# A decoder trunk on one core: conditioning units taken in groups of two to four, with projection granules between their loads and their matmuls

## The chip, the core and the metric

The kernel runs on one core of a Trainium2 chip. A core has five engines that run side by side and wait for each other through semaphores: TensorE (PE in the profile; its weight loads are PEld), VectorE (DVE), ScalarE (ACT), GpSimd (POOL) and SyncE (SP), which here issues most DMA transfers. The metric is the device time of one execution in microseconds (us), lower is better. Times are medians of several runs; the profile shows one execution.

## What is computed

One step of a decoder layer for 256 prompt tokens and 8 sequences of 4 sample tokens, 288 token columns in all, width 2048, in fp32. A vector `c` for each sequence (9 in all) conditions the layer:

```python
mod = jax.nn.silu(c) @ P['w_ada'] + P['b_ada']
sh1, sc1, gt1, sh2, sc2, gt2 = [m[:, None, :] for m in jnp.split(mod, 6, axis=-1)]
xn = rmsnorm(x, P['g_norm1']) * (1.0 + sc1) + sh1
mix, st = mixer(xn, states[l], P)
x = x + gt1 * mix
xn = rmsnorm(x, P['g_norm2']) * (1.0 + sc2) + sh2
x = x + gt2 * (jnp.square(jax.nn.relu(xn @ P['w_ff1'])) @ P['w_ff2'])
```

`w_ada` is 2048 x 12288, so 100 MB are read for a product with nine rows. The mixer projects `xn` with `w_in` and splits the result among three branches: RG-LRU (a convolution, gates and a scan), GLA (gated linear attention with a state for each head) and mLSTM (a matrix memory for each head). Their outputs go through `w_br_*`, are weighted by sigmoid gates, summed, and projected by `w_out`. The MLP follows.

## The kernel before

**Layout.** Features lie on the partitions, tokens on the free axis. A k-tile is 128 features by 288 tokens.

**Projections.** `stream` (lines 146 to 169) multiplies one block of 512 output features. It is a generator with one step for each granule of two k-tiles: one load of 0.5 MB into a `raw` tile (line 153, issued by SP), a cast to a rounded `hi` on ACT (154), the remainder `lo` on DVE (155), and 24 matmuls: for 4 output tiles and 2 k-tiles the products hi by xh, hi by xl, lo by xh (161 to 163), in the reduced-width format fp32r. `raw`, `hi` and `lo` have three tiles each. A block holds four PSUM banks, and its `evac` empties them.

**Conditioning.** `cond_product` (lines 205 to 222) multiplies rows of a weight matrix as the moving operand with the nine columns of silu(c) as weights, in plain fp32. One unit is a load of up to 2048 columns of one k-tile (1 MB for `ada`; 0.75 MB for the shift product) and its matmuls (line 216), four at 32 columns of the array each, so that the four column groups of the array work on four parts of the output. A unit's tile comes from `raw_tile` (198): a list `slots["ids"]` names the big slots that are free in the stage, with `None` for a tile of its own. At the end of a product the result is transposed on DVE (193) and finished by small vector operations at high priority.

`fillers` (272) strings the products together: the second half of SC1, SH1, `shift_product` (249; what SH1 adds to the three projection blocks that were run before it was there), GT1, SH2, SC2, GT2. `run` (171) takes a projection's generator through its granules and after some of them takes one step of `fillers`, by the pattern `pace["every"]`: (1,) after every granule, (1, 0) after every second, (1, 0, 0) after every third, () never. One step is one unit: its load and its matmuls. `drain` (283) takes steps until a product is done.

**Order of the stages.** Norm 1 and the first half of SC1; three blocks of `B_Q` over the first eight k-tiles, then over the last eight (lines 395 to 400, a step per granule); `drain("sh")` and the addition of the shift (401 to 403); the fourth block and two blocks for RG-LRU (406 to 410, every second granule); RG-LRU (442 to 508); a narrow stream of 8 granules and two gate blocks (512 to 523); `drain("cor")` (722); GLA (572 on); the first merge (every third granule) and two blocks `B_MX`; mLSTM; the second merge (no steps); two blocks `B_MO`, the third merge and the output projection (every third granule); norm 2; the MLP. The order of instructions on each engine is laid out ahead of time by a scheduler with a timing model: what comes first in the program has priority, and what is not ready is passed by what is. Loads and casts of `stream` have high priority, so they run ahead as far as their tiles allow. Each engine, and SP with its loads, then takes its instructions strictly in that order.

Of the kernel before, what the change touches and what calls it, by code (L numbers as in the profile page):

```python
# [25 lines left out]
NPRE = 3  # blocks of the projections before sh1  # L26

# name -> width of the constant (by shape only) and parameter columns
# [19 lines left out]
# blocks of 512 columns in the packed input projection  # L48
# [4 lines left out]
def trunk(ctx, tc, io):  # L53
# [35 lines left out]
    # ---- constants, parameters  # L89
# [25 lines left out]
    def resets(t, val, one, step):  # L115
        """scan coefficients: val where a segment starts (each step prompt tokens; each sample), one elsewhere"""
        G.memset(t, one)
        G.memset(t[:, 0:NP:step], val)
        G.memset(t[:, NP:N:TS], val)
        return t  # L120

    def head_bcast(p, r, w=N):
        """p[:, h * w ...] for one head at a time: the head's row of r on all partitions"""
# [4 lines left out]
    # ---- streamed weights  # L128
# [3 lines left out]
    def weight_tile(kind):  # L132
        """1024 columns: of the kind's ring, or what stands in for it: a slot or a tile of the states' ring"""
# [12 lines left out]
    def stream(w, blk, act, kt, evac, g0=0, width=512, ahead=True, k0=0):  # L146
        """k-tiles k0..kt-1; act: k -> (hi, lo); generator with a step per granule"""
# [30 lines left out]
    # ---- conditioning: silu(c) @ w_ada + b_ada  # L178
# [4 lines left out]
    silc = cp.tile([P, KT * 9 + 23], F32, tag="silc", name="silc")  # 9 columns a k-tile; read 32 at a time  # L183
# [6 lines left out]
    def by_feature(ps, h, n):  # L190
        """up to eight k-tiles' columns from the column groups: k-tile, 32 columns"""
# [4 lines left out]
    slots = {"ids": (None,), "n": 0}  # L196

    def raw_tile():
        slots["n"] += 1
        i = slots["ids"][slots["n"] % len(slots["ids"])]  # L200
        if i is None:
            return ring.tile([P, 2048], F32, tag="ag", name=nm("ag"))
        return flat(slot(i))[:, 0:2048]

    def cond_product(load, each, cols, stat, finish):
        """columns of w (natural order) times 9 columns of stat (k -> AP of 32 columns): features m * 128 + 32 j + f in the
        array's column group j; a load brings what each of some k-tiles takes"""
        ps = pa.tile([P, 512], F32, tag="pa", name=nm("pa"))
        for q in range(KT // each):
            raw = raw_tile()  # L210
            load(raw, q)
            for i in range(each):
                k = each * q + i
                v = raw[:, cols * i:cols * i + cols].rearrange("p (m j f) -> p j m f", j=4, f=32)
                for j in range(4):
                    T.matmul(ps[32 * j:32 * j + 32, 0:cols // 4], stat(k), v[:, j], start=k == 0, stop=k == KT - 1)  # L216
            if q < KT // each - 1:
                yield
# [5 lines left out]
    def ada_finish(kind):  # L224
        def finish(h, pv):
            o = mod[:, kind, 8 * h:8 * h + 8, :]
            V.tensor_tensor(out=o, in0=pv[:, :, 0:9], in1=bada[:, kind, 8 * h:8 * h + 8].unsqueeze(2).to_broadcast([P, 8, 9]), op=ALU.add)
            if kind in (SC1, SC2):  # g * (1 + sc)
# [9 lines left out]
    def ada(kind):  # L238
        def load(raw, k):
            Q.dma_start(raw.rearrange("p (h m) -> p h m", h=2), wada[kind, :, k].rearrange("h p m -> p h m"))  # L240
        return cond_product(load, 1, 2048, silu_c, ada_finish(kind))

    def ada_half(kind, h):
        """eight of the k-tiles of one kind"""
        def load(raw, q):
            Q.dma_start(raw.rearrange("p (k m) -> p k m", k=2), wada[kind, h, 2 * q:2 * q + 2].rearrange("k p m -> p k m"))
        return cond_product(load, 2, 1024, silu_c, lambda _, pv: ada_finish(kind)(h, pv))

    def shift_product(dst, nb):
        """the tiles of dst += sh1 @ w_in's nb blocks, for each token by its sequence"""  # L250
        def load(raw, k):
            Q.dma_start(raw[:, 0:512 * nb].rearrange("p (b m) -> p b m", b=nb),
# [33 lines left out]

    fill = fillers()

    # ---- normalisation over the features (on partitions and tiles)
    def sumsq(ps, x, k, s):  # L290
        """ps += the squares of x summed over its features; s gathers those of the first twelve k-tiles"""
# [19 lines left out]
    def smp(a):  # the samples' columns, by sequence  # L311
        return a[..., NP:N].rearrange("p k (b t) -> p k b t", b=NB)

    def modulate(xg, rs, k0, fk, xh, xl, xr):
        """k-tiles k0..k0+3 of x (xg) -> hi and lo of x * rstd * f"""
# [945 lines left out]
```

## Time and profile before

| | us |
|---|---|
| median of 3 runs | 2061.9 |
| lowest, highest | 2055.35, 2066.22 |
| the profiled execution, span from its first to its last instruction | 2058.2 |

The profile gives for the profiled execution no time besides its span, so the median is set against that. How to read its rows: a row of the timeline has the start in us, the duration, the engine, the line of the kernel, the operation, the tile written and the tiles read, the shape, and how many instructions of that kind were merged into the row. A bracket at its end says how long the engine had been idle and what ended that. Matmul rows overlap, since the next one starts while the last one is in flight, so starts say more than durations. One fp32 matmul leaves two records, so a unit of four matmuls shows as x8. Tile names: `pa` is the conditioning product in PSUM, `ag` and `s` the tiles its loads go to, `silc` the silu(c) columns, `mod` the SH1 columns, `mm` a projection's PSUM bank, `xh`, `xl` the two parts of the activations.

### The profile page before, as it was taken

To read this page: it belongs to the slowest core of one execution; us is meant where nothing else is said; L and a number is where in the kernel's file an instruction comes from. 1 tells how busy PE (TensorE), PEld (TensorE's weight loads), DVE (VectorE), ACT (ScalarE), POOL (GpSimd) and SP (SyncE) were. 2 spreads that over 40 slices of the span, in tenths; PEclk is the share of its full clock that TensorE was granted. 3 is DMA by queue.
4 is the path that set the end of the run, shared out by engine and by line. 5 is a ranking of instruction groups with operands and counts; after the bars stand their busy time and mean duration, and the time that the engine had idled before them with its cause. 6 is when DMAs were issued, how large, how long until landed. Compare 5 with 4: busy or idle time off the path is not lost.

```text
span 2058.2 us, 35340 instructions
## 1 busy us (share of the span) xinstructions
PE 2000.3 (97%) x14834; PEld 1824.4 (89%) x14834; DVE 1031.4 (50%) x1406; ACT 802.4 (39%) x1099; POOL 302.0 (15%) x342
## 2 busy tenths in 40 slices
PE   6999999999999999999999999999999999999997
PEld 4778778877889788889998989999999999999997
DVE  4354655354644366454444465434545444454565
ACT  3323465332435332244333344444343434343434
POOL 0120111021202223101111242101010101010102
PEclk8999999999999999999999999999999999999999
DMA  9988685377663257777778755555555555555552
GB/s 386 356 316 308 207 298 180 132 243 265 213 235 126 83 187 233 250 251 272 246 252 303 235 187 162 166 170 166 166 163 167 167 166 164 166 165 168 166 167 98
DMA packets 120959, 429.60 MB, mean 209 GB/s; under 512 B 11600, under 2 KB 13808, under 8 KB 120672
## 3 DMA queue, kind: packets, MB, share of 16 engines
q1 hardware_dynamic: 111728, 393.59, 56.4%
q0 software_dynamic: 7920, 29.04, 4.0%
q10 hardware_dynamic: 1152, 4.72, 0.6%
q8 instruction: 116, 1.90, 0.4%
q14 instruction: 43, 0.35, 0.0%
HBM read 410.49 MB, written 16.81 MB: 208 GB/s over the span
## 4 chain that ended last, share of the span: by engine, by line
PE 78%; DMA 2%; DVE 1%; issue 1%; POOL 1%; ACT 0%; DVEq 0%; SPq 0%; POOLq 0%
PE mm L161 24%; PE mm L163 23%; PE mm L162 23%; PE pa L216 3%; DMA st<-mC 1%; DMA ag<-wada 1%; DVE lo L155 0%; PE px L658 0%; PE pi L974 0%; PE px L931 0%; PE pi L535 0%; PE px L125 0%; PE px L980 0%; PE px L555 0%; DMA o_C_s<-st 0%
## 5 line engine op out<-in xcount | busy, mean ns | idle before, releaser
L155 DVE TENSOR_TENSOR lo<-raw,hi 128x1024 fp32r<-128x1024 f32 (+1 forms) x424 | 543.0, 1283 | 616.9 <-ACT hi L154 603.7
L154 ACT ACTIVATE hi<-raw 128x1024 fp32r<-128x1024 f32 (+1 forms) x424 | 442.9, 1046 | 801.5 <-PE mm L162 663.2
L161 PE MATMUL mm<-xh,hi 128*128 128x288 f32 x2168 | 645.4, 300 | 12.0 <-ACT xh L341 5.5
L162 PE MATMUL mm<-xl,hi 128*128 128x288 f32 x2168 | 641.3, 297 | 1.2 <-DVE xl L342 1.2
L163 PE MATMUL mm<-xh,lo 128*128 128x288 f32 x2168 | 630.2, 297 | 1.2 <-DVE lo L155 1.2
L161 PEld LDWEIGHTS mm<-xh,hi 128*128 128x128 f32 x2168 | 406.9, 188 | 67.5 <-issue 37.8
L163 PEld LDWEIGHTS mm<-xh,lo 128*128 128x128 f32 x2168 | 404.6, 189 | 13.4 <-issue 8.1
L162 PEld LDWEIGHTS mm<-xl,hi 128*128 128x128 f32 x2168 | 408.5, 188 | 8.8 <-issue 6.9
L162 PE MATMUL mm<-s,hi 128*128 128x288 f32 x1176 | 348.1, 296 | 0.0
L161 PE MATMUL mm<-s,hi 128*128 128x288 f32 x1176 | 347.6, 297 | 0.0
L163 PE MATMUL mm<-s,lo 128*128 128x288 f32 x1176 | 345.0, 295 | 0.0
L161 PEld LDWEIGHTS mm<-s,hi 128*128 128x128 f32 x1176 | 220.6, 188 | 13.6 <-issue 11.8
L163 PEld LDWEIGHTS mm<-s,lo 128*128 128x128 f32 x1176 | 220.9, 188 | 2.4 <-issue 2.2
L162 PEld LDWEIGHTS mm<-s,hi 128*128 128x128 f32 x1176 | 221.3, 188 | 1.2 <-issue 0.9
L1102 POOL TENSOR_TENSOR t<-t 128x288 f32<-128x288 f32 x64 | 62.6, 989 | 638.9 <-ACT t L1101 638.9
L161 PE MATMUL mm<-s,st 128*128 128x288 f32 x488 | 143.9, 296 | 0.0
L162 PE MATMUL mm<-s,st 128*128 128x288 f32 x488 | 143.3, 294 | 0.0
L154 ACT ACTIVATE st<-s 128x1024 fp32r<-128x1024 f32 x80 | 84.7, 1059 | 131.0 <-PE mm L162 86.9
L161 PE MATMUL mm<-xh,st 128*128 128x288 f32 x408 | 120.5, 297 | 0.2 <-DVE xl L1088 0.2
L162 PE MATMUL mm<-xl,st 128*128 128x288 f32 x408 | 120.1, 295 | 0.0
L161 PEld LDWEIGHTS mm<-s,st 128*128 128x128 f32 x488 | 91.7, 188 | 0.8 <-ACT t L296 0.8
L162 PEld LDWEIGHTS mm<-s,st 128*128 128x128 f32 x488 | 91.9, 188 | 0.0
(369 smaller groups left out, 2104.6 us busy)
## 6 DMA issues: line engine op xcount, KB each, us to landing
raw<-win SPq DMA_DIRECT2D x192, 512.0 KB, 4.4
raw<-wf SPq DMA_DIRECT2D x176, 512.0 KB, 3.4
ag<-wada SPq DMA_DIRECT2D x57, 1024.0 KB, 6.1
s<-wf SPq DMA_DIRECT2D x80, 512.0 KB, 3.5
s<-wada SPq DMA_DIRECT2D x39, 1024.0 KB, 8.3
raw<-wout SPq DMA_DIRECT2D x32, 512.0 KB, 4.4
s<-win SPq DMA_DIRECT2D x11, 768.0 KB, 7.2
st<-mC POOLq DMA_DIRECT2D x16, 514.0 KB, 4.6
```

The source lines that it names most:

```text
L154: S.activation(hi, raw, AF.Copy)
L155: V.tensor_tensor(out=lo, in0=raw, in1=hi.bitcast(F32), op=ALU.subtract)
L161: T.matmul(pss[m][:, :N], hi[:, kk, ms], xh, start=k == k0, stop=False)
L162: T.matmul(pss[m][:, :N], hi[:, kk, ms], xl, start=False, stop=False)
L163: T.matmul(pss[m][:, :N], lo[:, kk, ms], xh, start=False, stop=k == kt - 1)
L216: T.matmul(ps[32 * j:32 * j + 32, 0:cols // 4], stat(k), v[:, j], start=k == 0, stop=k == KT - 1)
L1102: G.tensor_tensor(out=r, in0=r, in1=r, op=ALU.mult)
```

## The change

`cond_product` no longer takes one unit per step. It takes `slots["group"]` units at once: it issues their loads, the last unit's first, so that the load of the unit whose matmuls come first is the last one; then it yields `slots["after"]` times, that is, it lets so many steps pass (granules of projections, where each takes a step); then it issues the matmuls of all the units in order. With `after` 0 it yields behind each unit as before. A new function `feed` sets tiles, group and distance for what follows and first lets a group whose loads have been issued finish.

```diff
-    slots = {"ids": (None,), "n": 0}
+    slots = {"ids": (None,), "n": 0, "group": 1, "after": 0, "loaded": False, "done": 0}
...
         if i is None:
-            return ring.tile([P, 2048], F32, tag="ag", name=nm("ag"))
-        return flat(slot(i))[:, 0:2048]
+            return [ring.tile([P, 2048], F32, tag="ag", name=nm("ag"))]
+        if i == "st":
+            return [sp.tile([P, 1028], F32, tag="st", name=nm("st"), bufs=2)[:, 0:1024] for _ in range(2)]
+        return [flat(slot(i))[:, 0:2048]]
...
-        for q in range(KT // each):
-            raw = raw_tile()
-            load(raw, q)
-            for i in range(each):
-                k = each * q + i
-                v = raw[:, cols * i:cols * i + cols].rearrange("p (m j f) -> p j m f", j=4, f=32)
-                for j in range(4):
-                    T.matmul(ps[32 * j:32 * j + 32, 0:cols // 4], stat(k), v[:, j], start=k == 0, stop=k == KT - 1)
-            if q < KT // each - 1:
+        q = 0
+        while q < KT // each:
+            n = min(slots["group"], KT // each - q)
+            raws = [raw_tile() for _ in range(n)]
+            for i in reversed(range(n)):
+                load(raws[i], q + i)
+            slots["loaded"] = True
+            for _ in range(slots["after"]):
+                yield
+            for raw in raws:
+                for i in range(each):
+                    k = each * q + i
+                    w = cols // len(raw)
+                    for h, r in enumerate(raw):
+                        v = r[:, w * i:w * i + w].rearrange("p (m j f) -> p j m f", j=4, f=32)
+                        for j in range(4):
+                            T.matmul(ps[32 * j:32 * j + 32, h * w // 4:(h + 1) * w // 4], stat(k), v[:, j], start=k == 0 and h == 0,
+                                     stop=k == KT - 1, skip_group_check=len(raw) > 1)
+                q += 1
+            slots["loaded"] = False
+            slots["done"] += 1
+            if not slots["after"] and q < KT // each:
                 yield
...
+    def feed(ids, group, after):
+
+        slots.update(ids=ids, group=group, after=after)
+        n = slots["done"]
+        while slots["loaded"] and slots["done"] == n:
+            next(fill, None)
```

A tile named `"st"` is a pair of tiles of the ring that GLA and mLSTM load their states into; such a unit has two loads and eight matmuls of half the width.

The settings along the program:

```diff
-    slots["ids"] = 2, 5, 6, 7, None
+    slots.update(ids=(2, 5, 6, 7, None), group=2, after=2)
...
-    pace["every"] = (1, 0)
-    slots["ids"] = 6, 7, None
+    feed((0, 1, 3, 4, 5, 6, 7, None), 4, 3)
...
+    drain("cor")
+    feed((6, 7, "st", None), 4, 4)
...
+    pace["every"] = ()
     run(stream(io["wsm"], 0, act1, KT, lambda m, p: S.copy(sm, p), width=P))
+    pace["every"] = (1,)
...
-    drain("cor")
-    slots["ids"] = None,
+    pace["every"] = ()
+    feed((None,), 1, 0)
     ygla = gla()
...
-    pace["every"] = (1, 0, 0)
     merge(0, ylru, io["wbl"])
...
     merge(1, ygla, io["wbg"])
-    pace["every"] = (1, 0, 0)
+    pace["every"] = (1, 0, 0, 0)
...
-    slots["ids"] = 8, 9, None
+    feed((8, 9, None), 3, 4)
+    pace["every"] = (1,)
...
-    for _ in range(3):
-        next(fill, None)
-    pace["every"] = ()
+    feed((None,), 1, 0)
```

Counted through, the products now stand so. SC1's second half and SH1: pairs, two granules between loads and matmuls. The shift product: a pair, three fours and a pair, with three granules between, in the fourth block and RG-LRU's two blocks. GT1: four fours behind it in the same blocks, the last one's matmuls behind the last granule. SH2: four fours, with four granules between, in the two gate blocks. From GLA to the second merge: none. SC2: one unit every fourth granule in `B_MO` and the third merge. GT2: five threes and a single in the first three blocks of the output projection, the single's matmuls ahead of the MLP.

More of the change, by code (lines that the diff above doesn't have):

```diff
@@ L239, in load @@
         def load(raw, k):
-            Q.dma_start(raw.rearrange("p (h m) -> p h m", h=2), wada[kind, :, k].rearrange("h p m -> p h m"))
+            if len(raw) == 1:
+                Q.dma_start(raw[0].rearrange("p (h m) -> p h m", h=2), wada[kind, :, k].rearrange("h p m -> p h m"))
+                return
+            for h, r in enumerate(raw):
+                Q.dma_start(r, wada[kind, h, k])
         return cond_product(load, 1, 2048, silu_c, ada_finish(kind))
@@ L245, in load @@
         def load(raw, q):
-            Q.dma_start(raw.rearrange("p (k m) -> p k m", k=2), wada[kind, h, 2 * q:2 * q + 2].rearrange("k p m -> p k m"))
+            Q.dma_start(raw[0].rearrange("p (k m) -> p k m", k=2), wada[kind, h, 2 * q:2 * q + 2].rearrange("k p m -> p k m"))
         return cond_product(load, 2, 1024, silu_c, lambda _, pv: ada_finish(kind)(h, pv))
@@ L251, in load @@
         def load(raw, k):
-            Q.dma_start(raw[:, 0:512 * nb].rearrange("p (b m) -> p b m", b=nb),
+            Q.dma_start(raw[0][:, 0:512 * nb].rearrange("p (b m) -> p b m", b=nb),
                         io["win"][B_Q:B_Q + nb, k // 2, :, 512 * (k % 2):512 * (k % 2) + 512].rearrange("b p m -> p b m"))
@@ L1089, in trunk @@
             E.tensor_tensor(out=l[:, NP:N], in0=f[:, NP:N], in1=h[:, NP:N].bitcast(F32), op=ALU.subtract)
-    slots["ids"] = None,
     facc = (slot(6), slot(7))
```

## The prediction

> **What bounds the kernel now.** I read the page's totals first, then its chain of work, then the timeline of TensorE around the conditioning matmuls.
>
> ```profile
> span 2058.2 us, 35340 instructions
> PE 2000.3 (97%) x14834; PEld 1824.4 (89%) x14834; DVE 1031.4 (50%) x1406; ACT 802.4 (39%) x1099; POOL 302.0 (15%) x342
> PE 78%; DMA 2%; DVE 1%; issue 1%; POOL 1%; ACT 0%; DVEq 0%; SPq 0%; POOLq 0%
> ```
>
> TensorE is the bound: every other engine is half idle, and the chain lies 78% on PE and 2% on DMA. A busy share of 97% says little about what that time buys, though, since a matmul counts as busy while it is in flight. So I price a conditioning unit (one load and its matmuls, line 216) by starts, not by durations.
>
> ```profile
> 963.44 0.29 PE L163 MATMUL mm<-s,lo 128*128 128x288 f32 x1
> 963.66 1.07 PE L216 MATMUL pa<-ag,silc 128*32 128x512 f32 x8
> 964.66 0.40 PE L161 MATMUL mm<-s,hi 128*128 128x288 f32 x1
> 964.90 0.29 PE L162 MATMUL mm<-s,hi 128*128 128x288 f32 x1
> ...
> 1129.00 0.29 PE L163 MATMUL mm<-s,lo 128*128 128x288 f32 x1
> 1129.22 1.06 PE L216 MATMUL pa<-s,silc 128*32 128x512 f32 x8
> 1130.11 1.04 PE L216 MATMUL pa<-ag,silc 128*32 128x512 f32 x8
> 1131.08 0.40 PE L161 MATMUL mm<-s,st 128*128 128x288 f32 x1
> 1131.31 0.30 PE L162 MATMUL mm<-s,st 128*128 128x288 f32 x1
> ```
>
> Columns: start, duration, engine, line, what is written from what, count. Streamed matmuls follow each other by 0.133 us (0.24 just behind a unit, the first of the two disturbed steps). From 963.44 to 964.90 are 1.46 us; two undisturbed steps would be 0.27; a lone unit costs **1.19**. From 1129.00 to 1131.31 are 2.31, less 0.27: two units in one visit cost **2.04**. So a unit is 0.85 and each visit, the change from streamed to conditioning matmuls and back, adds 0.34.
>
> A visit that is cut in two is dearer still:
>
> ```profile
> 434.29 1.06 PE L216 MATMUL pa<-ag,silc 128*32 128x512 f32 x6
> 435.27 0.40 PE L161 MATMUL mm<-s,hi 128*128 128x288 f32 x1
> ...
> 436.26 1.05 PE L216 MATMUL pa<-ag,silc 128*32 128x512 f32 x2
> 437.23 0.54 PE L161 MATMUL mm<-s,hi 128*128 128x288 f32 x2
> ```
>
> Six of the eight records of one unit take 0.98 until the next start, and the other two 0.97: the four column groups run side by side, so a part costs as much as the whole. A cut adds about 1.2.
>
> **What grouping removes.** Units are counted from the code, visits and cuts from the timeline. First and last visits of the products:
>
> ```profile
> 49.17 1.07 PE L216 MATMUL pa<-ag,silc 128*32 128x256 f32 x16
> 133.69 1.06 PE L216 MATMUL pa<-s,silc 128*32 128x512 f32 x8
> 139.12 0.85 PE L216 MATMUL pa<-s,mod 128*32 128x384 f32 x8
> 149.69 0.85 PE L216 MATMUL pa<-s,mod 128*32 128x384 f32 x8
> 150.35 0.83 PE L216 MATMUL pa<-ag,mod 128*32 128x384 f32 x8
> 246.76 0.85 PE L216 MATMUL pa<-s,mod 128*32 128x384 f32 x8
> 251.16 1.06 PE L216 MATMUL pa<-s,silc 128*32 128x512 f32 x8 [1.94 <-DMA s<-wada]
> 436.26 1.05 PE L216 MATMUL pa<-ag,silc 128*32 128x512 f32 x2
> 451.30 1.05 PE L216 MATMUL pa<-ag,silc 128*32 128x512 f32 x2
> 546.50 1.07 PE L216 MATMUL pa<-ag,silc 128*32 128x512 f32 x8 [1.44 <-DMA ag<-wada]
> 867.71 1.07 PE L216 MATMUL pa<-ag,silc 128*32 128x512 f32 x8 [1.31 <-DMA ag<-wada]
> 1071.11 1.06 PE L216 MATMUL pa<-ag,silc 128*32 128x512 f32 x8
> 1222.36 1.56 PE L216 MATMUL pa<-ag,silc 128*32 128x512 f32 x8 [2.48 <-DMA ag<-wada]
> 1250.71 1.07 PE L216 MATMUL pa<-ag,silc 128*32 128x512 f32 x8
> ```
>
> - SC1's second half and SH1 (49.17 to 133.69): 24 units in 21 visits, one cut. After, pairs: 12 visits. 9 x 0.34 plus 0.85 = 3.9.
> - Shift product (139.12 to 246.76): 16 units in 12 visits, three cuts. A unit of 384 columns is 0.66 (149.69 to 150.35). After, 2+4+4+4+2: 5 visits. 7 x 0.34 + 3 x 0.66 = 4.4.
> - GT1 (251.16 to 436.26): 16 units in 18 visits, two of them cuts. After, 4 visits: 14 x 0.34 + 2 x 0.85 = 6.5.
> - SH2 (451.30 to the one behind 867.71): 20 visits, four cuts. After, 4 visits: 16 x 0.34 + 4 x 0.85 = 8.8.
> - SC2: 16 single visits before and after, one unit every fourth granule: nothing.
> - GT2 (1071.11 to 1250.71): 15 visits, three cuts. After, five threes and one: 6 visits. 9 x 0.34 + 3 x 0.85 = 5.6.
>
> Sum 29.2. I take off 5 for cuts that remain (four at 1.2; before there are nine in the 48 units of GT1, SH2 and GT2, and a longer visit offers as many places to be cut, but now between plain projections, where the run of 16 lone units of SC2 has none). Of the 3.9 in the first stage I credit half, because DMA is nearly full there (below). That leaves **22**.
>
> TensorE also waits for single late loads: 1.94, 1.44 and 1.31 in the rows above, 4.7 together; with reversed loads the first matmul of a group waits for the last load, so a group waits once. The 2.48 at 1222.36 lies beside the norm that holds the MLP's first matmul, and counts nothing. I credit the **4.7** and charge new waits separately.
>
> **What moves, and what it collides with.** GT1 and SH2 leave GLA and the merge for the projections (lines 404 to 410 and 512 to 523). TensorE does the same units there, so the move itself is neutral; the DMA is not.
>
> ```profile
> 25.00:50.00 25.00, 14.81 (x112) 10.55 (x112) 13.26 (x22) 5.57 (x7) 2.90 (x6) 0.66 1.02 409
> 49.00:134.00 85.00, 85.00 (x686) 64.28 (x688) 29.71 (x39) 26.48 (x35) 9.51 (x7) 1.00 0.97 363
> 153.00:240.00 87.00, 86.50 (x644) 79.14 (x648) 39.39 (x49) 32.72 (x44) 0.55 (x1) 1.00 0.73 247
> 240.00:306.00 66.00, 61.48 (x412) 44.17 (x406) 42.37 (x61) 42.74 (x66) 16.94 (x22) 1.00 0.82 300
> ```
>
> The last three columns are granted clock, DMA share, GB/s. DMA has carried 409 GB/s, and 363 at a share of 0.97 (374 when full). The stage behind the shift, 153 to 240, runs at 247 today. After, it holds 24 granules of 0.52 MB, 14 shift units of 0.79 and 16 GT1 units of 1.05, with RG-LRU's 1.15 MB at its end: 41.5 MB. TensorE needs 24 x 24 x 0.133 = 77, plus 14 x 0.66 + 4 x 0.34 = 10.6, plus 16 x 0.85 + 4 x 0.34 = 15: about 102 us. DMA needs 102 at 409 GB/s and 111 at 374, so between 0 and 9 is lost; I take **6**, nearer to 374, since that is a long stretch and the 409 is a short one.
>
> The gates' stage (B_GATE, 16 granules, all of SH2, the 8 narrow granules): 26 MB, 64 to 70 us of DMA, against TensorE's 51 + 15 + 6 and the RG-LRU products: enough on average. But four tiles carry groups of four, so the next four loads (4.2 MB, 10.3 to 11.2 us, plus landing) start only when the last matmul of the group is done, and TensorE reaches the next group after four granules, 12.8 us. Each of three groups may wait 0 to 3 us: **3**. GT2's threes take 8.4 us of 12.8 and cost nothing.
>
> SP issues in order, so a projection's load stands behind a burst of four. How far ahead these loads run decides what that costs:
>
> ```profile
> 205.28 1.06 ACT L154 ACTIVATE hi<-raw 128x1024 fp32r<-128x1024 f32 x1 [2.14 <-PE mm L162]
> raw<-win SPq DMA_DIRECT2D x192, 512.0 KB, 4.4
> SPq L153 <- DVE lo L155: 117.7, 53, 5.3
> ```
>
> The cast waits for TensorE to free a tile, so weights are ready in time. With three raw tiles and three cast ones, the load of granule g is issued when granule g-3 has been cast, one cast (1.06 on ACT and about as long on DVE, 2.3 us) behind TensorE's start of g-5; it must have landed one cast ahead of the start of g. That is 5 x 3.2 - 2.3 - 2.3 = 11.4 us of cover for a landing of 4.4. A burst of 10.3 to 11.2 ahead of it makes 15: up to 3.6 late. I count it inside the 6 and the 3, where the same bytes are already charged.
>
> RG-LRU's weights and its state now wait for slots 3 and 5 (GT1's third group). What covers it:
>
> ```profile
> 301.67 1.17 ACT L341 ACTIVATE s<-s 128x1152 fp32r<-128x1152 f32 x1 [1.11 <-DVE s L499]
> 332.75 0.98 ACT L518 ACTIVATE t<-mm 128x288 f32<-128x288 f32 x3
> ```
>
> RG-LRU ends at 304, the gates behind which it hides at 332: 28 us of slack, and SH2 adds 15. Nothing is charged; beyond 43 us late, GLA would start late one for one. GLA's state tiles, now lent to SH2, are free again long before GLA's samples.
>
> SH1's last pair stands behind the last granule of its stage, where one unit stood; the shift and the next block wait for it: one unit more, **1**. The other edits (no steps in the 8 narrow granules, none from GLA to the second merge, one step in four behind it) only say where units stand and are in the counts.
>
> **Sum.** -22 - 4.7 + 6 + 3 + 1 = -16.7 on the profiled 2058.2, about 2041.5. The median of the runs, 2061.9, lies 3.7 above the span, and I keep that difference: **2045**.
>
> **The rivals.** *DMA holds only the 363 of the first stage.* Then that stage gains nothing (-20), the stage behind the shift takes 114 instead of 102 (12) and the gates wait 3 a group (9): -20 - 4.7 + 21 = -4, about 2058, no change that can be told (0.5%, some 10 us, is what a measurement of this kernel can tell from none). For it: 0.97 at 363 over 85 us. Against: the 409. The Trainium skill, "DMA: Bandwidth & Descriptors", Specifications, gives about 358 GB/s as what HBM lends one core; by that the stage would take 116 us and the sum be -2. The trace's 409 is above it, so I hold it less likely.
>
> *The bursts starve the projections.* One queue issues all loads in order; where its head waits for a conditioning tile that TensorE has yet to release, projection loads stand behind it, and TensorE then waits for them. The eight bursts of GT1 and SH2 decide: the gain of 26.7 is gone when each costs 3.3. The landing of 15 against the cover of 11.4 gives 3.6, and a group that is itself 3 late 6.6; in the middle between 3.3 and 6.6, 5.0 each, the sum is -26.7 + 40 = +13: 2075. For it: loads on SP wait for line 216 already. Against: two sets of tiles for GT1.
>
> *Everything fits.* DMA gives 400 or more, no cuts remain: -29.2 - 4.7 = -34, 2028.
>
> **How the numbers follow.** The forecast has 0.46, everything fits 0.16, DMA at 363 0.25, starving 0.13. Faster by over 0.5% are the first two, 0.62; within it 0.25; slower 0.13. The range runs from 2028 to 2066: below lies only a gain that I have no row for, above most of the starving case.
>
> **What would show it.** Right: visits of 32 records at line 216 with about 3.4 us from first start to the next streamed start, some 45 to 50 visits instead of 102 behind 46 us, and a stage behind the shift of 102 to 111 us at over 370 GB/s. Wrong: groups cut by streamed matmuls; ACT's casts idle for raw tiles on the way into the gates; TensorE idle ahead of a group for more than 3 us; RG-LRU's end after that of the gates.

## The result, and the profile after

The changed kernel takes 2077.4 us in the median of 8 runs (2074.45 to 2084.24), before in the same session 2063.3 (2055.35 to 2070.61): **1.0073** of before, 95% interval 1.0052 to 1.0094. It is slower by some 14 us. The forecast of 2045 was wrong in size and in sign, and the time lies above the range.

The page of the changed kernel's profile, the lines that answer to those of before:

```profile
span 2082.5 us, 35429 instructions
PE 1999.0 (96%) x14866; PEld 1837.7 (88%) x14866; DVE 1027.0 (49%) x1406; ACT 801.4 (38%) x1099; POOL 311.5 (15%) x342
PE 85%; DMA 3%; issue 2%; DVE 2%; ACT 1%; POOL 0%; DVEq 0%; POOLq 0%; ACTq 0%
```

TensorE is as busy as before in sum (1999 us for 2000) in a span that is 24 longer. The profiled execution is the slowest of the eight, so some 7 of those 24 us belong to it alone. (Line 228 is the conditioning matmul now, 216 before; the loads are at 257, 260, 266 and 272.)

The visits came out at the predicted price. Timeline of TensorE, changed kernel:

```profile
101.92 0.29 PE L163 MATMUL mm<-xh,lo 128*128 128x288 f32 x1
102.14 1.06 PE L228 MATMUL pa<-ag,silc 128*32 128x512 f32 x8
103.03 2.76 PE L228 MATMUL pa<-s,silc 128*32 128x512 f32 x24
105.71 0.40 PE L161 MATMUL mm<-xh,hi 128*128 128x288 f32 x1
105.95 0.29 PE L162 MATMUL mm<-xl,hi 128*128 128x288 f32 x1
```

From 101.92 to 105.95 are 4.03, less 0.27: 3.76 for four units; 4 x 0.85 + 0.34 is 3.74. What was gained so was lost between the visits. Windows of before and of the changed kernel (columns: width, busy time and count of PE, PEld, DVE, ACT, POOL, granted clock, DMA share, GB/s), each from the start of the projections to the shift, on to the narrow granules, and on to the end of the gates:

```profile
45.00:149.00 104.00, 103.18 (x819) 80.75 (x819) 44.75 (x60) 31.78 (x40) 18.06 (x12) 1.00 0.95 350
149.00:239.00 90.00, 88.33 (x665) 79.53 (x664) 42.43 (x53) 33.54 (x43) 2.24 (x4) 1.00 0.72 242
239.00:331.00 92.00, 87.47 (x595) 67.84 (x595) 59.95 (x81) 58.62 (x85) 23.57 (x26) 1.00 0.76 274
```

```profile
45.00:160.00 115.00, 103.04 (x825) 83.00 (x824) 49.26 (x71) 34.63 (x42) 19.59 (x12) 0.97 0.94 360
160.00:275.00 115.00, 110.86 (x862) 86.40 (x861) 40.60 (x62) 31.00 (x40) 4.13 (x5) 0.99 0.91 346
275.00:375.00 100.00, 86.11 (x592) 70.47 (x590) 50.91 (x61) 53.68 (x81) 17.68 (x20) 0.95 0.67 237
```

Width less PE busy is TensorE's idle time: 0.8 + 1.7 + 4.5 = 7.0 us before, 12.0 + 4.1 + 13.9 = **30.0** after. The granted clock, 1.00 in all three before, falls to 0.97, 0.99 and 0.95, which over 115, 115 and 100 us is up to 9.6 us more. How an idle gap does that:

```profile
241.12 1.92 PE L228 MATMUL pa<-s,silc 128*32 128x512 f32 x16
245.38 0.40 PE L161 MATMUL mm<-xh,hi 128*128 128x288 f32 x1 [2.33 <-ACT hi L154]
...
246.27 0.44 PE L161 MATMUL mm<-xh,hi 128*128 128x288 f32 x1
246.50 0.44 PE L162 MATMUL mm<-xl,hi 128*128 128x288 f32 x1
246.88 1.94 PE L228 MATMUL pa<-s,silc 128*32 128x512 f32 x8
248.74 0.61 PE L163 MATMUL mm<-xh,lo 128*128 128x288 f32 x1
249.15 0.44 PE L161 MATMUL mm<-xh,hi 128*128 128x288 f32 x1
```

TensorE waits 2.33 us for a cast; 0.9 us after it is back the step between streamed matmuls grows from 0.13 to 0.23, and a single unit with the two steps around it takes 2.65 (246.50 to 249.15) instead of 1.46, 1.8 times as long. The Trainium skill, "TensorE: Matmul & The Clock Gate", Part 1, describes such a drop: a window of about 3.4 us that counts as idle sets the clock to half, and as long a busy one restores it. The trace comes near the factor (2.65 to 1.46), but the gap that the profile shows here is only 2.33 us. Not every gap of that size has this effect: in before 2.23 us at 302.03 and 2.54 us at 336.12 left the granted clock at 1.00 in the windows around them (295 to 310 and 331 to 345).

**What ended the waits.** By what ended each gap, the 30.0 us fall into these parts. Three gaps, 10.9 us together, end with a late cast or a late remainder whose weights had landed 6 to 9 us before (245.38, 315.06, 330.29). 6.2 us end with a late load of a conditioning unit. 4.8 us end with a PSUM bank that DVE emptied late, behind the vector work of the shift (131.04, 137.06). 3.3 us are the gap at 74.88, where a load landed and SC1's second half came in at about the same time. 2.4 us end with a late load of a projection (122.30, 259.74), and 2.3 are small gaps. The rows behind the first part:

```profile
242.30 2.07 ACT L444 ACTIVATE s<-s,par 128x256 f32<-128x256 f32 x4 [11.06 <-PE pa L228]
244.28 1.99 ACT L154 ACTIVATE hi<-raw 128x1024 fp32r<-128x1024 f32 x2
...
309.30 3.73 ACT L511 ACTIVATE s<-s,lam 128x288 f32<-128x288 f32 x7
...
313.96 1.99 ACT L154 ACTIVATE hi<-raw 128x1024 fp32r<-128x1024 f32 x2
315.06 0.61 PE L161 MATMUL mm<-xh,hi 128*128 128x288 f32 x1 [5.20 <-ACT hi L154]
...
324.02 5.11 DVE L527 TENSOR_TENSOR_SCAN s<-s,s 128x576 f32<-128x576 f32 x4
329.04 2.34 DVE L155 TENSOR_TENSOR lo<-raw,hi 128x1024 fp32r<-128x1024 f32 x2
330.29 0.40 PE L163 MATMUL mm<-xh,lo 128*128 128x288 f32 x1 [3.34 <-DVE lo L155]
```

At 242.30 ACT has been idle for 11.06 us. RG-LRU's convolution (line 444) writes big slot 4, and conditioning units hold that slot until they have been multiplied. The two casts behind it in ACT's order had their weights since 235.39 and 239.23, by the landings in the trace. In before that convolution starts at 209.9 and waits for nothing. At 313.96 two casts come behind RG-LRU's activations, though their loads had landed at 305.65 and 306.93, and at 329.04 the remainders come behind RG-LRU's scan on DVE.

For the experiments I cut every run by its streamed matmuls, 24 to a granule, since their number and order by stage stay the same: 0 to 24 is the stage ahead of the shift, 24 to 48 the fourth block and RG-LRU's two, 48 to 76 the narrow granules, the gates, GLA and the first merge's first ten granules, 76 to 132 the rest of that merge and `B_MX`. Times in us, each row from the timeline of one profiled execution, which can lie up to 10 us off the median of its kernel. A stage ends with its last streamed matmul, so the shift itself lies in 24 to 48. Visits are counted up to granule 132 (four of them ahead of 42 us):

| kernel | 0-24 | 24-48 | 48-76 | 76-132 | sum | visits | of before, 95% interval |
|---|---|---|---|---|---|---|---|
| before | 110.2 | 90.2 | 143.6 | 246.1 | 590.1 | 73 | 1 |
| changed | 121.3 | 114.3 | 142.4 | 225.2 | 603.2 | 37 | 1.0073 (1.0052-1.0094) |
| c_s1 | 103.7 | 99.8 | 145.1 | 244.0 | 592.6 | 66 | 0.9993 (0.9981-1.0004) |
| c_s1a1 | 116.4 | 86.7 | 137.7 | 249.5 | 590.3 | 69 | 1.0019 (1.0003-1.0035) |
| c_xy | 119.6 | 108.2 | 147.5 | 225.2 | 600.5 | 41 | 1.0056 (1.0037-1.0075) |
| c_g | 110.1 | 91.4 | 143.7 | 247.0 | 592.2 | 73 | 1.0013 (1.0003-1.0023) |
| e_fwd | 120.5 | 114.3 | 140.8 | 226.7 | 602.3 | 37 | 1.0081 (1.0064-1.0098) |
| e_gate1 | 104.0 | 138.9 | 136.3 | 225.2 | 604.4 | 48 | 1.0081 (1.0063-1.0100) |
| e_gate2 | 114.8 | 108.6 | 160.0 | 219.1 | 602.5 | 38 | 1.0056 (1.0037-1.0075) |
| e_gate12 | 103.6 | 132.3 | 160.3 | 219.1 | 615.3 | 41 | 1.0122 (1.0101-1.0143) |
| b_mix | 103.5 | 131.6 | 161.3 | 219.1 | 615.5 | 41 | 1.0110 (1.0087-1.0133) |
| e_pool | 104.3 | 130.4 | 135.8 | 233.0 | 603.5 | 44 | 1.0078 (1.0050-1.0106) |
| e_pair | 103.2 | 114.0 | 163.2 | 215.1 | 595.5 | 54 | 1.0038 (1.0024-1.0051) |
| b_pair | 104.0 | 114.4 | 157.7 | 220.4 | 596.5 | 59 | 1.0020 (1.0001-1.0039) |
| b_pair1 | 108.6 | 108.5 | 144.2 | 232.1 | 593.4 | 67 | 1.0023 (1.0006-1.0039) |
| b_ppool | 103.3 | 115.8 | 157.7 | 223.1 | 599.9 | 58 | 1.0049 (1.0026-1.0072) |
| v_place | 110.1 | 90.2 | 137.4 | 254.6 | 592.3 | 73 | 1.0041 (1.0022-1.0061) |
| v_move | 110.8 | 104.7 | 179.9 | 234.8 | 630.2 | 107 | 1.0038 (1.0024-1.0051) |
| v_gt1 | 103.3 | 109.6 | 149.9 | 252.8 | 615.6 | 73 | 1.0084 (1.0053-1.0115) |

Stages differ in how many units lie in them, so a single column says little; the sum compares, since 31 to 35 units are left after granule 132 in all but v_move (10) and v_gt1 (23). By it the changed kernel loses 13.1 us, nearly all of the median's 14. The rest of the profiled span's 24 lies for the most part in mLSTM and the second merge (granules 132 to 192, 299.7 us for 291.1), where the change does next to nothing: that stage took 290.1 in e_gate1 and 295.7 in e_fwd, whose conditioning stands there as in the changed kernel.

### The profile page after: what moved, and what is told of

It reads as the page before. It is cut to its first block, busy times and chain, and to the rows that moved or that the text cites. A ratio compares the mean times of both kernels' runs of the same rounds, so it can differ in the third digit from the quotient of the medians.

```text
span 2082.5 us, 35429 instructions
## 1 busy us (share of the span) xinstructions
PE 1999.0 (96%) x14866; PEld 1837.7 (88%) x14866; DVE 1027.0 (49%) x1406; ACT 801.4 (38%) x1099; POOL 311.5 (15%) x342
## 4 chain that ended last, share of the span: by engine, by line
PE 85%; DMA 3%; issue 2%; DVE 2%; ACT 1%; POOL 0%; DVEq 0%; POOLq 0%; ACTq 0%
PE mm L161 26%; PE mm L162 25%; PE mm L163 25%; PE pa L228 3%; DMA st<-mC 2%; DVE lo L155 1%; DMA s<-wada 1%; PE px L688 0%; PE pi L1003 0%; PE px L960 0%; PE pi L565 0%; DMA s<-win 0%; PE px L125 0%; PE px L585 0%; ACT hi L154 0%
## 5 line engine op out<-in xcount | busy, mean ns | idle before, releaser
L161 PEld LDWEIGHTS mm<-xh,hi 128*128 128x128 f32 x2168 | 411.5, 190 | 56.2 <-issue 21.6
L162 PEld LDWEIGHTS mm<-xl,hi 128*128 128x128 f32 x2168 | 413.3, 191 | 10.8 <-issue 9.2
L163 PEld LDWEIGHTS mm<-xh,lo 128*128 128x128 f32 x2168 | 408.2, 191 | 13.9 <-DVE lo L155 7.3
L154 ACT ACTIVATE st<-s 128x1024 fp32r<-128x1024 f32 x80 | 84.7, 1059 | 129.8 <-PE mm L162 86.7
```

The source lines that it names most:

```text
L154: S.activation(hi, raw, AF.Copy)
L161: T.matmul(pss[m][:, :N], hi[:, kk, ms], xh, start=k == k0, stop=False)
L162: T.matmul(pss[m][:, :N], hi[:, kk, ms], xl, start=False, stop=False)
L163: T.matmul(pss[m][:, :N], lo[:, kk, ms], xh, start=False, stop=k == kt - 1)
```

## The experiments

All parts of the change apart first. **c_s1** is before with the pairs for SC1 and SH1 only, **c_xy** before with the new shift product, GT1 and SH2 only, **c_g** before with GT2 in threes only (the settings of `pace` that go with them are left out here):

```diff
-    slots.update(ids=(2, 5, 6, 7, None), group=1, after=0)     # c_s1
+    slots.update(ids=(2, 5, 6, 7, None), group=2, after=2)
...
-    pace["every"] = (1, 0)                                     # c_xy
-    feed((6, 7, None), 1, 0)
+    feed((0, 1, 3, 4, 5, 6, 7, None), 4, 3)
...
+    drain("cor")
+    feed((6, 7, "st", None), 4, 4)
...
-    feed((8, 9, None), 1, 0)                                   # c_g
+    feed((8, 9, None), 3, 4)
+    pace["every"] = (1,)
```

> The kernel before with the change in the first stage alone: SC1's second half and SH1 in pairs, two granules between loads and matmuls; everything behind the shift as before. Theory A (conditioning loads get ahead of the projections' loads on a DMA that is already full there, and TensorE then waits for weights): 7 to 12 us slower than before, and all of the loss lies ahead of the 24th granule. Rival B (the loss of 10 us in that stage comes from loads of later products that slipped forward, which this kernel does not have): within 2 us of before. My prediction's term for this stage: 1 to 3 us faster.

Measured 0.9993, not told from before: 6.5 us won ahead of granule 24, all given back behind it.

> The kernel before with the change for the shift product, GT1 and SH2 alone (fours, three or four granules between loads and matmuls, none from GLA to the second merge); SC1, SH1 and GT2 one unit at a time as before. Theory A: the 20 us that fewer visits save are given back as waits for projection weights and late groups; within 5 us of before. Rival B (early loads of these products are what slows the first stage): 5 to 12 us slower, with the loss ahead of the 24th granule. My prediction's terms: -19.7 + 2.5 for cuts - 4.7 + 9 = 13 us faster.

Measured 1.0056: the larger part of the loss is here, and 9.4 us of it lie ahead of granule 24, where this kernel issues the same single units as before. What is new there is on the SyncE queue. Its timeline in the changed kernel:

```profile
17.66 2.07 SPq L153 DMA_DIRECT2D raw<-win  x2
20.23 2.89 SPq L260 DMA_DIRECT2D st<-wada  x2
26.43 5.46 SPq L266 DMA_DIRECT2D s<-wada  x3
32.83 0.37 SPq L272 DMA_DIRECT2D s<-win  x1
...
45.29 0.38 SPq L272 DMA_DIRECT2D s<-win  x1
```

Line 260 is a unit of SH2, which the program has some 250 us later, line 272 the shift product. The scheduler places a load where its tile is free and the queue idle, however late it stands in the program; the new tiles were free at once. c_xy's own queue shows the same row of line 260, at 20.18.

> The kernel before with the change in the output projection alone: what is left of GT2 there in threes, three or four granules between loads and matmuls, every granule a step. In this stage DMA has room (249 GB/s before). Theory A: between 3 us faster and 3 us slower, as the profile of the changed kernel shows 3.5 lost there; a loss would have to show as projections' casts that wait for weights. My prediction's term: 5 us faster.

Measured 1.0013, no gain. The timeline of the changed kernel shows why, at GT2:

```profile
1146.04 1.07 PE L228 MATMUL pa<-s,silc 128*32 128x512 f32 x8
1146.92 1.02 PE L228 MATMUL pa<-ag,silc 128*32 128x512 f32 x2
1150.45 1.04 PE L228 MATMUL pa<-ag,silc 128*32 128x512 f32 x2
1152.41 0.62 PE L228 MATMUL pa<-ag,silc 128*32 128x512 f32 x2
```

A group of three is cut into several visits. GT2's 16 units make 15 visits in before, 11 in the changed kernel and 13 in c_g, where I had counted 6.

**e_fwd** is the changed kernel with `for i in range(n)` for `reversed(range(n))`:

> The changed kernel with each group's loads in forward order. Theory A: within 3 us of the changed kernel, 12 to 17 slower than before, since a group waits for all its loads either way and the bytes are the same. Rival C (the reversed order starts each group late, because its first load goes to the tile that is released last): 6 us or more faster than the changed kernel.

Measured 1.0081 and the same stages within 1.6 us: the order of loads inside a group decides nothing.

**Early loads held back.** e_gate1 makes the shift product's loads wait for SH1's result (first line below), and SH2's first pair of state tiles too; e_gate2 makes SH2's first four loads wait for the end of the narrow granules (the other lines); e_gate12 has the lines below; b_mix is e_gate12 with GT2 as in before:

```diff
+            V.tensor_copy(raw[0][:, 0:1], mod[:, SH1, 0, 0:1])   # shift product, ahead of each load
...
+            if kind == SH2 and k < 4:
+                for r in raw:
+                    V.tensor_copy(r[:, 0:1], sm[:, 0:1])
```

> After, with every load of the shift product made to wait for SH1's result, and the first pair of state tiles (SH2's) for the same: nothing but SC1 and SH1 is loaded ahead of about 121 us, in the order of before. Theory H (loads of later products that slip forward into the full DMA of the first stage cost it some 10 us): the stage ahead of granule 24 ends 8 to 15 us earlier than in the changed kernel, the narrow granules still lose some 10 to 15, and the time is 2063 to 2069, within 0.3% of before. Rival S (the bursts themselves starve the projections, wherever they stand): the stage ahead of granule 24 stays within 3 us of the changed kernel's, the time is 2073 to 2080.

> After, with SH2's first four loads made to wait for the end of the narrow granules (a copy from their result). Theory H: the two early loads of the shift product stay (one early unit of SH2 goes), so the stage ahead of granule 24 loses 5 to 10 us as it did, but the eight narrow granules take 50 to 56 us instead of 65.6, and SH2 lies in the gates; the time is 2063 to 2070. Rival S: the burst only moves, what the narrow granules gain the gates lose, and the time is 2073 to 2080.

> After, with both holds: the shift product's loads not ahead of SH1's result, SH2's first four not ahead of the end of the narrow granules. Theory H: both losses go and the saving of fewer visits is left, 2050 to 2060, that is 0.994 to 0.998 of before. Rival S: 2070 or more.

> The kernel with both holds, and GT2 in single units as before (the threes alone cost 1.0013 of before). Theory H: 1 to 4 us below the kernel with both holds, 2048 to 2058. Rival S: 2068 or more.

Measured 1.0081, 1.0056, 1.0122 and 1.0110. Theory H is not borne out as the cause of the net loss. The hold does what it says, the stage ahead of granule 24 takes 104.0 instead of 121.3, but granules 24 to 48 then take 138.9 instead of 114.3, and the sum is the same. With both holds it is worst of all. The bytes have to come before GLA in any case; loaded early they cost the first stage, loaded late the second. A rival is not excluded: a held load stands in SyncE's queue ahead of projections' loads, so a hold may cost something by itself. SyncE waits for the copy into a held tile twice in e_gate1, 7.3 us in all, and twice in e_gate12, 8.9 us. What of this reaches TensorE was not taken apart.

**How they come.** In e_gate12 all of the shift product and GT1 is loaded in the stage for which I had predicted 102 to 111 us. It took 132 from the end of the stage before, and 125 from its first granule on, which is the stretch that I had priced; and not because DMA was full. Windows of e_gate12 and, below it, of **e_pair**, where the shift product and GT1 come in pairs on four tiles instead of fours on eight:

```profile
143.00:275.00 132.00, 115.62 (x856) 87.48 (x855) 56.06 (x101) 36.51 (x46) 10.77 (x11) 0.95 0.85 321
```

```profile
142.00:256.00 114.00, 107.19 (x810) 84.47 (x810) 54.73 (x94) 33.92 (x42) 10.88 (x11) 0.97 0.92 342
```

```diff
-    feed((0, 1, 3, 4, 5, 6, 7, None), 4, 3)
+    pace["every"] = (1, 1, 0)
+    feed((0, 1, 6, 7), 2, 1)
```

> The kernel with both holds, with the shift product and GT1 in pairs, one pair in one and a half granules, on four tiles instead of fours on eight: the same bytes and units in the same 24 granules, in smaller bursts. Theory Q: these granules take 113 to 124 us instead of 132 although there are more visits (16 for 9, 2.4 us), and the time is 2068 to 2077. Theory D: 128 us or more, 2081 to 2092.

Measured 1.0038 after 1.0122. Six units of GT1 slip into the narrow granules, so the whole of 24 to 132 must be compared: 492.3 for 511.7 us, **19 us less** with the same units and bytes and 13 visits more. The edit changes more than the size of a burst, though: four tiles for eight (slots 3, 4 and 5 stay free for RG-LRU), one granule for three between loads and matmuls, and the rate. Which of these did it was not separated. The profile's table of DMA issues in these windows, median time from issue to landing in the last column, for before, the changed kernel, e_gate12 and e_pair:

```profile
raw<-win SPq DMA_DIRECT2D x21, 512.0 KB, 4.7
```

```profile
s<-wada SPq DMA_DIRECT2D x18, 1024.0 KB, 9.4
raw<-win SPq DMA_DIRECT2D x20, 512.0 KB, 7.4
```

```profile
s<-wada SPq DMA_DIRECT2D x14, 1024.0 KB, 16.9
raw<-win SPq DMA_DIRECT2D x21, 512.0 KB, 10.1
```

```profile
s<-wada SPq DMA_DIRECT2D x14, 1024.0 KB, 7.4
raw<-win SPq DMA_DIRECT2D x21, 512.0 KB, 6.6
```

A projection's load lands in 10.1 us among fours and in 6.6 among pairs. ACT's casts wait for it. The profile's waits in the same windows (us in total, times, the longest), e_gate12 and e_pair:

```profile
ACT hi L154 <- DMA raw<-win: 54.9, 13, 15.6
```

```profile
ACT hi L154 <- DMA raw<-win: 10.8, 4, 4.4
```

TensorE's own waits in these windows are 16.4 and 6.8 us. In both some 6.7 of them stand at the shift. The rest, in e_gate12 alone, ends with late loads of conditioning groups (5.2), with casts and remainders (3.6) and with a conditioning matmul (0.8).

Is it the order in SyncE's queue? **e_pool** is e_gate12 with these loads issued by GpSimd:

```diff
-            Q.dma_start(raw[0][:, 0:512 * nb]
+            G.dma_start(raw[0][:, 0:512 * nb]
```

> The kernel with both holds, with the loads of the shift product, GT1 and SH2 issued by GpSimd instead of SyncE; nothing else differs. With both holds the 24 granules behind the shift took 132 us at 321 GB/s and a DMA share of 0.85. Theory Q (loads of a group that wait for their tiles at the head of SyncE's one queue keep the projections' loads waiting): those granules take 112 to 122 us, and the time is 2066 to 2075. Theory D (the stage has too many bytes to load, in whatever order): 128 us or more there, and 2081 to 2090.

Measured 1.0078. Granules 24 to 48 take 130.4, as with one queue: there the order is not the cause. The projections' loads do land sooner and the casts wait less, from 143 to 275 in e_pool:

```profile
raw<-win SPq DMA_DIRECT2D x21, 512.0 KB, 7.6
```

```profile
ACT hi L154 <- DMA raw<-win: 27.0, 8, 9.4
```

TensorE gains nothing by it: behind the shift 7.2 us of its waits end with late loads of conditioning groups and 1.7 with casts and remainders. What e_pool wins it wins in the gates (48 to 76: 135.8 for 160.3), and 14 us of it are given back behind them (233.0 for 219.1). So the order in one queue did cost in the gates of this kernel, with its holds; in the changed kernel, without them, it was not tested. The Trainium skill, "DMA: Bandwidth & Descriptors", Issuing engines are not separate DMA queues, says that transfers run on the same 16 DMA engines and interleave, whichever engine issued them; that agrees with the 130.4. With the DMA share at 0.85 in both kernels, the fours also leave DMA partly idle; that this is while all tiles are full and none is released is argued, not shown. How much is the long landing and how much such pauses was not taken apart.

> The kernel with both holds and pairs for the shift product and GT1 (1.0038 of before), with the conditioning loads of the shift product, GT1 and SH2 issued by GpSimd. With fours that took 1.0122 to 1.0078, all of it in the gates. If the same holds here, 0.997 to 1.001 of before; if what GpSimd gained was the fours' only, 1.002 to 1.006.

Measured 1.0049: with pairs, GpSimd's queue gains nothing over 1.0038.

> As the one before, and SH2 in pairs over the 16 granules of the gates on three tiles, GT2 in single units as in before. Theory Q: granules 24 to 48 as in the kernel before this one, the gates' 16 granules 3 to 8 us shorter than the 75 of the kernel with both holds; 2058 to 2070. Theory D: 2075 or more.

Measured 1.0020, the lowest of the kernels that keep the move, but not told from e_pair's 1.0038: the intervals overlap, GT2 is back in single units as well, and what 48 to 76 gains (157.7 for 163.2) is given back behind it (220.4 for 215.1).

**Moving and grouping apart.** v_move issues a single unit behind every granule from the shift to GLA, v_place pairs units where they stood, v_gt1 moves GT1 alone, in pairs, with SC1 and SH1 in pairs too and the shift product held behind SH1's result:

```diff
-    pace["every"] = (1, 0)                   # v_move
+    pace["every"] = (1,)
...
-    feed((6, 7, None), 1, 0)                 # v_place
+    feed((6, 7, None), 2, 2)
...
+    pace["every"] = (1, 1, 1, 1, 0)          # v_gt1
+    feed((0, 1, 6, 7, None), 2, 2)
```

> Before, with one conditioning unit behind every granule from the shift to GLA instead of behind every second: nothing is grouped, some 24 units move ahead of GLA as singles, on before's three tiles. Theory P: the stretch from granule 24 to 66 takes 20 us or more beyond before's 182 less what its added units cost (24 at 1.19, 29), GLA and the merge give back 20 to 29, and the time is 1.002 to 1.008 of before. Theory B: single loads harm nothing, the time is 0.996 to 1.001 of before.

Measured 1.0038. It has done 24 units more by granule 132 than before, in 34 visits more; at 0.85 and 0.34 that is 32 of its 40 us, so 8 are lost, as many as in the median, with no group in it. Its window over the narrow granules and gates:

```profile
254.00:369.00 115.00, 106.08 (x691) 76.30 (x690) 60.76 (x71) 64.29 (x93) 24.27 (x25) 0.94 0.84 304
```

8.9 us idle for 4.5 in before's 92 us of the same granules, at a clock of 0.94 for 1.00. Moving the units to this place costs by itself. Late loads are not what TensorE waits for there: 5.7 us end with casts and remainders and 2.8 with an activation of RG-LRU, and no cast waits for a load of `win` in this window.

> Before, with the shift product and the part of GT1 that lies ahead of GLA in pairs at the same rate (a pair every four granules, on before's three tiles); nothing is moved, SC1, SH1, SH2, SC2 and GT2 stay as in before. About 12 visits and some of five cuts fewer, 4 to 8 us by the prices of the trace. Theory P (grouping itself gains, moving GT1 and SH2 ahead of GLA is what loses): 2052 to 2057, 0.996 to 0.999 of before. Theory B (any burst, of two too, costs the projections about what the visits save): 0.999 to 1.003 of before.

Measured 1.0041, but it tells little of grouping: it makes 73 visits up to granule 132, as before does, since the scheduler had put before's shift units together already (11 units in 7 visits). Its twelve runs spread from 2060.5 to 2078.1 with the profiled one the fastest, so its row doesn't show what made the median of 2069.9; that stays open.

> Before, with pairs where DMA has room: SC1 and SH1 in pairs, the shift product held behind SH1's result, shift product and GT1 in pairs, one in two and a half granules, on to the end of the gates; SH2, SC2 and GT2 in single units, SH2 through GLA and the merges where GT1's rest and SH2 were. A third less is loaded between granules 24 and 48 than with all of GT1 there. Both theories: that stage takes 95 to 105 us; if only the place and the size of the bursts made the changed kernel slow, the time is 2045 to 2057, below before by some 20 visits at 0.34 us; if pairs cost here too, it is 2060 or more.

Measured 1.0084, against what both theories expected. Eleven units more are done by granule 132, in as many visits as before; at 0.85 that is 9 of 25.5 us. Here too the moved units cost more than where they were.

**The first stage.** c_s1's 6.5 us could have been lost because SH1 came last: its transposes stand at 146.3 us for 135.0 before. c_s1a1 brings SH1 forward, b_pair1 is b_pair with SC1 and SH1 in single units:

```diff
-    slots.update(ids=(2, 5, 6, 7, None), group=2, after=2)
+    slots.update(ids=(2, 5, 6, 7, None), group=2, after=1)
...
-    pace["every"] = (1,)
+    pace["every"] = (1, 1, 0)
```

These are the lines of c_s1a1 against c_s1; b_pair1 has `group=1, after=0` in the first.

> The kernel with pairs for SC1 and SH1 only (0.9993 of before; there granule 24 was reached 6.2 us earlier than in before, but SH1 was done at 146.3 instead of 135.0, behind it), with one granule between loads and matmuls and a pair in one and a half granules instead of two. Theory L (the pairs' lead was given back because SH1 came last and the shift stood open behind it): SH1 done at 125 to 138, granules 24 to 32 take 33 to 36 us instead of 39.6, 2053 to 2058, 0.996 to 0.999 of before. Rival F (DMA is full up to there, so whatever is loaded earlier only changes places): granule 24 comes later by what SH1 comes earlier, 0.999 to 1.002.

> The kernel with pairs for the shift product, GT1 and SH2, both holds and GT2 single (1.0020 of before), with SC1 and SH1 in single units as in before. Theory L: SH1 done at 133 to 138, granule 24 at 149 as in before, granules 24 to 32 take 36 to 39 us instead of 44.0, and the time is within 2 us of that kernel's or up to 4 below it, 0.999 to 1.003. Rival F: 24 to 32 stays at 43 or more, 1.004 or more.

Measured 1.0019 and 1.0023. SH1 is done at 132.9 in c_s1a1, and granule 24 is reached 6.2 us later than before: rival F. In b_pair1 F's sign does not come: SH1 is done at 136.7 and granules 24 to 32 take 37.1 us instead of 44.0, as theory L had it, but the time, 1.0023 for 1.0020, gains nothing that can be told. Up to there DMA has a share of 0.90 to 0.95 in before, c_s1 and these two; that what one load gains another loses fits c_s1a1. The visits saved in that stage bring no gain that can be told. No kernel tried beats before; c_s1 equals it.

## Why the prediction was wrong

**The prices held, the count half.** With 0.85 a unit and 0.34 a visit, four units in a visit should take 3.74; they took 3.76. But I read visits from the grouping in the program. Behind 42 us there are 61 instead of the 45 to 50 expected, and 102 in before, because the scheduler places a group's matmuls apart (the rows of GT2 above). Up to granule 132 it is 37 for 73, 12 us. GT2's 5.6 came to nothing (c_g), and so did the 2 credited in the first stage (c_s1). The 1 charged for SH1's last pair was not due in the changed kernel, where SH1's transposes come at 121.0 us for 135.0 before. The 4.7 for late single loads didn't come either. Waits of the conditioning matmuls in the changed kernel:

```profile
PE pa L228 <- DMA s<-wada: 6.9, 7, 2.5
PE pa L228 <- DMA ag<-wada: 3.6, 2, 2.1
```

With 1.7 in two for `s<-win`, that is 12.2 us in 11 waits, for 13.3 in 9 before (6.7 and 6.6): larger groups waited as often and about as long.

**The step that failed** is the charge for TensorE's waits. I set DMA's sum against TensorE's sum over a stage and wrote 6, 3 and 1, less 4.7, so 5.3 us in all. For a burst ahead of a projection's load I wrote "up to 3.6 late. I count it inside the 6 and the 3, where the same bytes are already charged", and for RG-LRU, whose slots were lent out, "Nothing is charged". Up to granule 132 TensorE idles 18.3 us longer than before (30.0 in the changed kernel, none of it behind 375 us; in before the 7.0 and 4.6 more from 331 to 629). By stage that is 11.2 us more ahead of the shift, where I charged 1, 2.4 more behind it, where I charged 6, 9.4 more on to the end of the gates, where I charged 3, and 4.6 less behind them. On top comes what I had no term for: behind gaps the clock went to half for some us, up to 9.6 us in sum.

What the charge left out is of two kinds. The first is how the loads come. The same units cost 19 us less in pairs on four tiles than in fours on eight, and with all its loads inside it the stage priced at 102 to 111 took 125 in e_gate12, at a DMA share of 0.87 from 150 to 275. The row that I used, 4.4 us of landing, was the median of all 192 loads of that kind in the run. With DMA at 0.95 it was 7.3 already in before (45 to 149 us). It is 11.5 and 7.4 in the changed kernel's first two windows and 10.1 among e_gate12's fours, and of the 11.4 us of cover little is left. My row of a cast that waits for TensorE was one row; in the same stage of before (149 to 239) casts waited seven times for a load:

```profile
ACT hi L154 <- DMA raw<-win: 20.4, 7, 10.0
```

Even so, late loads of projections ended only 2.4 us of the changed kernel's waits, and those of conditioning units 6.2. The second kind is larger there. I asked whether RG-LRU ends in time, and not what stands behind it on ACT and DVE, which make the casts. 10.9 us are casts and remainders behind RG-LRU's work, and 2.3 of these come from a lent slot that held ACT for 11 us. What the changed kernel would take with only one of the two put right was not run.

Up to granule 132 the account is +18.3 idle time, up to +9.6 for the clock, -12.2 for visits, +1.7 for two units more: 17.4 for the 13.1 measured. The rest I didn't take apart; fewer cuts and a clock counted twice where TensorE is idle would both go that way. Against the forecast, the visits saved 10 us less than 22, the waits cost 13 more than 5.3, and the clock was missing. Two smaller terms were off as well: GT1 has three cuts, not two, and of the 3.7 us between span and median only 1.7 lie within one execution (2084.24 and 2082.5); the rest is spread between runs.

**A second wrong premise**: that loads stand where the program has them ("the next four loads start only when the last matmul of the group is done"). SH2's first was issued at 20 us. It moved 17 us between two stages and nothing in the sum, as e_gate1 shows, but it made the stages hard to foretell.

**What was right.** RG-LRU does end ahead of the gates (its scan ends at 329 us, the gates' last tanh at 376), so GLA didn't wait for it. The price of a group was right, and SC2 at nothing. The stage behind the shift, priced at 102 to 111 us, took 114 in the changed kernel with five units of SH2 more in it. GLA and the merge did give back what left them: 225.2 for 246.1. Of the rivals, "the bursts starve the projections" has the sign, and its 2075 lies near the 2077.4. That the number fits is luck: it put 40 us of waits against 26.7 saved, where at most 28 and 10.5 were measured. Its mechanism held only in part. I had put it on the order in SyncE's one queue; e_pool shows that this isn't it behind the shift, and that it had a part in the gates of a kernel with holds. The rival with DMA at 363 GB/s had the rate about right: the changed kernel's first two windows ran at 360 and 346, and 407 held only for a shorter stretch (75 to 125 us).

## What to carry to other kernels

When loads are moved or bundled, price the landing of all loads beside them under the new burst, not only the bytes over the stage: with the holds, fours on eight tiles cost 19 us more than pairs on four, though they save 13 visits. When a tile is lent to background work, ask which engine its next owner will hold up, and what stands behind it there: here two casts waited behind a convolution that waited for its slot. Moving units ahead of GLA gained nothing here, in fours, in pairs or one by one. Count visits in the order the scheduler lays out, not in the order of the program.

## What was not expected of the hardware

A gap of 2.33 us on TensorE was followed by some 3 us of a slower clock, in which a unit with the two steps around it took 2.65 us instead of 1.46; two gaps of about that size in before were not. The window of the changed kernel around it has a granted clock of 0.83:

```profile
240.00:250.00 10.00, 7.67 (x47) 4.06 (x47) 7.06 (x14) 3.97 (x6) 1.90 (x2) 0.83 1.02 409
```

And half-megabyte loads took 10.1 us to land, in the median, in a stretch where DMA was busy for only 0.85 of the time (e_gate12), for 4.7 at 0.72 (before).
